# A hybrid encoder on one core: 4 KB slots cut in halves, score rows without slots of their own in the prompt, eight subtractions moved to GpSimd, another pace for side work

## The chip, the cores and the metric

The kernel runs on one core of a Trainium2 chip. The metric is the time of one execution on the device in microseconds (us), taken as the median of three runs. Lower is better.

## The reference, cut to what matters

Two batches go through the same layer with the same weights: a prompt of 512 tokens and a sample of 1024 tokens, both 1024 wide, in float32.

```python
h = _rmsnorm(x, norm_attn_g)
z = h @ w_in                       # q, k, v and two conv halves: 512 + 256 + 1024 columns
a_out = _window_attn(q, k, v, ...) # 8 heads of 64, blocks of 128 with their neighbours,
                                   # m = max(scores, sink); p = exp(s - m)
                                   # denom = sum(p) + exp(sink - m)
c = ca * sigmoid(cb)
c = silu(_layernorm(_dwconv(c, 31 taps)))
x = x + concat([a_out, c]) @ w_out
h = _rmsnorm(x, norm_ffn_g)
u = _dwconv(h @ w_up, 3 taps)      # 5632 columns
x = x + (silu(u[..., :2816]) * u[..., 2816:]) @ w_down
y = _rmsnorm(x, norm_final_g)
```

## The kernel before, in words

A float32 product is made of three matmuls of rounded parts: each operand is split into a high part (`fp32r`, a cast on ScalarE, L142) and a low part (raw less high, a subtraction on GpSimd or VectorE, L143), and high x high, high x low and low x high are added up in PSUM (`proj`, L249 to L252; `out_half`, L648 to L650; `prod`, L1002 to L1004; down-projection, L1334 to L1336). A matmul here is 128x128 by 128x512.

The stages follow one another on TensorE (PE), with side work between:

- To about 95 us the prompt is normed, transposed and projected (`step(i, 0)`, 14 weight chunks of 128 columns). To about 290 us the sample follows with the same 14 chunks and two halves of 512 tokens each, 48 matmuls a chunk. Beside it runs the side job `prompt()`: the prompt's attention in 8 units (4 blocks, 2 groups of four heads; `scores`, L512 to L530, then `values`, L553 to L579), `conv_norm` for its four blocks (L606 to L631: transposes L612, statistics, a normed copy L618, transposes L624, swish) and its output projection.
- To about 683 us the prompt's FFN up-projection goes on in 22 steps (`ffn_step`; convolution taps on VectorE, L775; gate, L797 to L806, stored in the DRAM tiles `gt`). Its side job `sample()` is the sample's attention, 16 units, then the load and split of w_out in 16 pieces of 128x512 (`load_wo`, `split_wo`), then `conv_norm` of the first blocks.
- To about 830 us follows the sample's output projection (`out_blocks`): per block of 128 tokens two halves of 24 matmuls, an addition (L653), a store of the result (`x1d`, L656), a sum of squares (L659), and `scaled` (L900). The side jobs are 11 `pair_sums`: each loads two tiles of `gt` (L811, L812), makes four sums on GpSimd (L816 to L819) and stores four (L821, `gb`); and `conv_norm` of later blocks and `turned` (transposes of the normed rows, L925; high part L927; low part L878). Then come sums of w_up blocks (`sums_up`, subtractions at L878) and their splits (L988, L878).
- The sample's up-projection (to 1240 us) and down-projection follow.

**What sets the order.** The program is written with generators: `tick()` runs between matmuls and takes the next piece of the first side job whenever `pace["due"]` reaches 1; each tick adds `pace["rate"]`. The rates are the constants in L40 (RB for the in-projection of the sample, RD and RN for the FFN, RE for the output projection). A scheduler then orders the instructions of each engine statically, by its own estimate of the time at which each could run. All DMAs of this case are issued by SyncE's queue (SP), in order.

**Memory.** `Slots` (L60 to L92) hands out fixed places in SBUF by size: 15 q of 4096 bytes, 4 c of 4224, 61 h of 2048, 2 d of 2176 and 32 s of 64, per partition. A tile gets a free slot of the least size that holds it, the one longest free first. A tile of 2048 bytes therefore takes a whole q slot of 4096 when no h or d is free. A slot goes back when the last Python reference to its tile is dropped; the next tile in it waits until the reads and DMAs of the one before have ended.

**Score rows.** `sink_columns` takes four q slots for the whole of an attention (`score_rows`), each for two heads, with the negated sink logit in column 0 of each row. `scores` writes the negated and biased scores behind that column (L514), and the exponential (L523) reads the row with the sink's column, so that its accumulated sum is the denominator. The exponentials go into four tiles `p` that `values` then transposes.

Of the kernel before, what the change touches and what calls it, by code (L numbers as in the profile page):

```python
# [9 lines left out]
F32 = mybir.dt.float32  # L10
# [26 lines left out]

RA, RB, RBO, RD, RN, RE = 1.2, 0.8, 2.5, 0.8, 0.95, 1.4  # L40


CA, CB = 0.9, 0.4
# [4 lines left out]
SCB, SCD = "aapa", "aaap"  # L48


WOP, WOA, DW, DW2 = 1, 5, 2, 2
NE = 2
YN = 2
OB = "uc"
VG = 3
NW = 36
U0 = 2


class Slots:  # L60

    def __init__(self, pool, classes):
        self.pool, self.free, self.n = pool, [], 0
        for kind, (count, size) in classes.items():
            for i in range(count):
                self.free.append((f"{kind}{i}", size))

    def tile(self, shape, dt=F32, nbytes=4, among=None):  # L70
        need = nbytes
        for s in shape:
            need *= s
        fits = [s for s in self.free if s[1] >= need and (among is None or s[0][0] in among)]
        if not fits:
            raise RuntimeError(f"no slot for {need} bytes")
        least = min(s[1] for s in fits)
        slot = next(s for s in fits if s[1] == least)
# [13 lines left out]
        self.slots.free.append(self.slot)  # L92


@with_exitstack
def tile_hybrid_encoder(ctx: ExitStack, tc: tile.TileContext, xs, rel_bias, norm_attn_g, w_in,
                        attn_sink, conv_dw_w, conv_dw_b, conv_ln_g, conv_ln_b, w_out, norm_ffn_g,
# [9 lines left out]
    sb = Slots(big, dict(q=(15, 4096), c=(4, 4224), h=(61, 2048), d=(2, 2176), s=(32, 64)))  # L107
# [388 lines left out]
    def scores(u):  # L496
# [7 lines left out]
        off = (kts[0] - b + 1) * P  # L504
        q = qt.pop(u)
        negm, den = sm(GRP), sm(GRP)
        pr = []
        for j in range(GRP):
            h = kv * GRP + j
            sc = bank("attn")  # L510
            for L in range(2):
                nc.tensor.matmul(sc[:, :nk], q[:, j, :], kt[G["g"], kv][L][:, k0:k0 + nk],  # L512
                                 start=(L == 0), stop=(L == 1))
            nc.vector.tensor_tensor_reduce(  # L514
                out=row_of(h)[:, 1:1 + nk], in0=sc[:, :nk], in1=bias[h][:, off:off + nk], scale=-1.0,
                scalar=nsink[:, h:h + 1], op0=ALU.add, op1=ALU.min, accum_out=negm[:, j:j + 1])
            del sc
            if j == 1:
                yield 0.0

        for j in range(GRP):
            p = sb.tile([1 + 3 * P])
            nc.scalar.activation(p[:, :1 + nk], row_of(kv * GRP + j)[:, :1 + nk], AF.Exp, scale=-1.0,  # L523
                                 bias=negm[:, j:j + 1], accum_out=den[:, j:j + 1])
            pr.append(p)
        nc.vector.reciprocal(den[:], den[:])
        for j in range(GRP):
            eng = (SCB if G["g"] == 0 else SCD)[j]
# [1050 lines left out]
```

## Time and profile before

| what | value |
|---|---|
| median of three runs | 1574.94 us (1573.73 to 1581.71) |
| the profiled execution | 1579.13 us |
| its span, first to last instruction | 1577.3 us |
| mean granted clock of TensorE | 0.982 |
| instructions | 20139 |
| DMA, mean over the span | 144 GB/s |

A timeline row gives start and duration in us, engine, line, operation, tiles (out, then in, by their slot kinds: a, b, c, u and t are PSUM banks on the side of a matmul; q, c, d, h and s are slots in SBUF elsewhere), shape and count; in brackets stands the idle time of the engine ahead of it and what ended that. A row of waits gives the engine with its line, what it waited for, the total in us, how often, and the longest. PE is TensorE, DVE VectorE, ACT ScalarE, POOL GpSimd. A busy PE may run at a lower granted clock.

### The profile page before, as it was taken

The page shows a single profiled execution, that of the slowest core. Times are in us where ns is not written, and L with a number is a line of the kernel's source. Part 1 is how long each engine was busy: PE and PEld are TensorE (multiplying, and loading weights), DVE is VectorE, ACT ScalarE, POOL GpSimd, SP SyncE. Part 2 cuts the span into 40 slices and gives each one's busy share as a digit, 9 for nine tenths or more (in the row PEclk, how much of TensorE's full clock was granted, in tenths as well). Part 3 has the DMA queues.
Part 4 walks back from the last instruction along what each step waited for, and adds up shares of the span by engine and source line. Part 5 has one row for each costly group of instructions (what it writes and reads, how often), then busy time and mean ns, then how long its engine had stood idle before and what let it go on. Part 6 is the DMA issues. An engine that isn't in the chain of part 4 may idle for free. (4 is left out here: it accounts for less than half of the span.)

```text
span 1577.3 us, 20139 instructions
## 1 busy us (share of the span) xinstructions
PE 1517.2 (96%) x6843; PEld 1234.2 (78%) x6843; DVE 1155.5 (73%) x1604; ACT 794.6 (50%) x1396; POOL 711.6 (45%) x558
## 2 busy tenths in 40 slices
PE   8999999799999999899979999999999999999997
PEld 6787778587888888788867888888888788888885
DVE  7998577747888895745776787778876945668883
ACT  4635545435677786624344444544445533343354
POOL 6641334324667765746533555555555000003345
PEclk9999899899999999999989999999999999999999
DMA  7573235328343435778432333333331582356644
GB/s 227 159 193 94 69 107 160 100 96 252 105 129 127 131 124 160 222 231 273 147 110 67 99 103 100 101 100 100 105 119 57 191 303 77 117 158 221 216 151 160
DMA packets 228780, 227.17 MB, mean 144 GB/s; under 512 B 13268, under 2 KB 168348, under 8 KB 228549
## 3 DMA queue, kind: packets, MB, share of 16 engines
q1 hardware_dynamic: 228677, 225.88, 45.2%
q8 instruction: 54, 0.88, 0.2%
q14 instruction: 49, 0.40, 0.1%
HBM read 164.74 MB, written 62.14 MB: 144 GB/s over the span
## 5 line engine op out<-in xcount | busy, mean ns | idle before, releaser
L143 POOL TENSOR_TENSOR q<-q,q 128x1024 fp32r<-128x1024 f32 x71 | 172.2, 2431 | 115.4 <-ACT q L142 43.0
L878 DVE TENSOR_TENSOR h<-h,h 128x512 fp32r<-128x512 f32 (+2 forms) x202 | 155.9, 805 | 64.4 <-ACT h L882 25.6
L878 POOL TENSOR_TENSOR q<-q,q 128x512 fp32r<-128x512 f32 x82 | 114.2, 1404 | 152.9 <-ACT q L988 147.7
L1334 PE MATMUL w<-h,h 128*128 128x512 f32 x462 | 181.3, 392 | 0.5 <-DVE q L1121 0.5
L1335 PE MATMUL w<-h,h 128*128 128x512 f32 x462 | 181.3, 392 | 0.0
L1336 PE MATMUL w<-h,h 128*128 128x512 f32 x462 | 181.2, 392 | 0.0
L249 PE MATMUL u<-h,q 128*128 128x512 f32 x400 | 162.4, 406 | 6.5 <-DVE h L775 4.5
L250 PE MATMUL u<-h,q 128*128 128x512 f32 x400 | 159.6, 399 | 0.0
L252 PE MATMUL u<-h,q 128*128 128x512 f32 x384 | 152.4, 397 | 1.9 <-POOL q L143 1.8
L1002 PE MATMUL w<-h,q 128*128 128x512 f32 x372 | 147.7, 397 | 3.5 <-ACT h L1083 1.6
L1004 PE MATMUL w<-h,q 128*128 128x512 f32 x372 | 147.1, 395 | 0.6 <-POOL q L878 0.6
L292 DVE SCALAR_TENSOR_TENSOR c<-c,cvw,c 128x512 f32<-128x512 f32 x184 | 137.9, 750 | 2.5
L875 POOL TENSOR_TENSOR q<-q,q 128x1024 f32<-128x1024 f32 x12 | 32.9, 2752 | 236.9 <-DVE q L875 220.2
L1003 PE MATMUL w<-h,q 128*128 128x512 f32 x350 | 137.7, 393 | 0.0
L882 ACT CAST h<-h 128x512 fp32r<-128x512 f32 x120 | 71.8, 619 | 95.4 <-DVE h L878 41.2
L249 PE MATMUL b<-h,q 128*128 128x512 f32 x256 | 103.7, 405 | 1.9 <-DVE d L322 1.6
L142 ACT CAST q<-q 128x1024 fp32r<-128x1024 f32 x72 | 75.3, 1050 | 59.5 <-DMA q<-in_w_in 23.9
L1334 PEld LDWEIGHTS w<-h,h 128*128 128x128 f32 x462 | 86.8, 188 | 20.5 <-ACT h L882 0.9
L250 PE MATMUL b<-h,q 128*128 128x512 f32 x256 | 102.1, 399 | 0.0
L1336 PEld LDWEIGHTS w<-h,h 128*128 128x128 f32 x462 | 86.7, 188 | 19.6
L1335 PEld LDWEIGHTS w<-h,h 128*128 128x128 f32 x462 | 86.8, 188 | 19.5
L252 PE MATMUL b<-h,q 128*128 128x512 f32 x240 | 95.9, 400 | 0.0
(427 smaller groups left out, 3819.5 us busy)
## 6 DMA issues: line engine op xcount, KB each, us to landing
q<-in_w_up SPq DMA_DIRECT2D x88, 512.0 KB
ga<-q SPq DMA_DIRECT2D x64, 256.0 KB
h<-ga SPq DMA_DIRECT2D x57, 256.0 KB
q<-in_w_in SPq DMA_DIRECT2D x28, 512.0 KB
h<-in_w_down SPq DMA_DIRECT2D x52, 256.0 KB
q<-in_x_sample SPq DMA_DIRECT2D x15, 512.0 KB
h<-qsd SPq DMA_DIRECT2D x24, 256.0 KB
x1d<-q SPq DMA_DIRECT2D x11, 512.0 KB
```

What stands on the lines that cost most here:

```text
L143: (nc.vector if dve else nc.gpsimd).tensor_tensor(lo[:], raw[:], hi[:].bitcast(F32), op=ALU.subtract)
L249: nc.tensor.matmul(out, whi[:, kc, :], hi[:], start=(kc == 0), stop=False)
L250: nc.tensor.matmul(out, whi[:, kc, :], lo[:], start=False, stop=False)
L252: nc.tensor.matmul(out, wlo[:, kc, :], hi[:], start=False, stop=(kc == KC - 1))
L292: nc.vector.scalar_tensor_tensor(acc[:], src(t), w(t), acc[:], op0=ALU.mult, op1=ALU.add)
L878: (eng or nc.vector).tensor_tensor(out, a, b, op=ALU.subtract)
L1002: nc.tensor.matmul(out, whi[:, s], hi[:], start=(start and c == 0), stop=False, **go)
L1003: nc.tensor.matmul(out, whi[:, s], lo[:], start=False, stop=False, **go)
L1004: nc.tensor.matmul(out, wlo[:, s], hi[:], start=False, stop=(stop and c == 3), **go)
L1334: nc.tensor.matmul(out, sh[:, c], th[:], start=(p == 0), stop=False)
L1335: nc.tensor.matmul(out, sh[:, c], tl[:], start=False, stop=False)
L1336: nc.tensor.matmul(out, sl[:, c], th[:], start=False, stop=(p == NPAIR - 1))
```

## The change

Four things are changed.

1. **Halves.** When a 4-byte tile of at most 2048 bytes finds no free slot below 4096 bytes, a free q slot is cut into two `Half` tiles, if more than three q slots (`KEEP`) are free; else it takes a whole slot as before. Free halves are kept by type (`F32`, `F32R`), the last one freed is given out first, and the slot goes back when both are free.
2. **Score rows.** `sink_columns` is called for the sample's attention alone. In the prompt's, the scores go straight into the tile `p`, the exponential runs in place, and the sink's share is made apart: an addition of sink and negated maximum, an exponential (both 128x4) and an addition to the sum.
3. **DW2 = 0.** Of the 16 low parts of the sample's w_out, 8 were on VectorE (`m % 4 < 2`); now all 16 are on GpSimd.
4. **Pace.** The output projection of the sample's first four blocks (i = 4 to 7) runs with rate 2.2 and the next ones with RE = 0.9, where RE = 1.4 held throughout.

```diff
-RA, RB, RBO, RD, RN, RE = 1.2, 0.8, 2.5, 0.8, 0.95, 1.4
+RA, RB, RBO, RD, RN, RE = 1.2, 0.8, 2.5, 0.8, 0.95, 0.9
...
-WOP, WOA, DW, DW2 = 1, 5, 2, 2
+WOP, WOA, DW, DW2 = 1, 5, 2, 0
...
+KEEP = 3
...
+        if self.halved and nbytes == 4 and need <= 2048 and not any(s[1] < 4096 for s in fits):
+            halves = self.halves[dt]
+            if not halves and sum(s[0][0] == self.halved for s in fits) > self.keep:
+                slot = next(s for s in fits if s[0][0] == self.halved)
+                self.free.remove(slot)
+                self.n += 1
+                whole = Whole(self, slot, dt, self.pool.tile([P, 2, 512], dt, tag=slot[0], name=f"{slot[0]}_{self.n}", bufs=1))
+                halves += [(whole, 0), (whole, 1)]
+                whole = None
+            if halves:
+                return Half(*halves.pop(0), shape)
...
+class Half:
...
+    def __del__(self):
+        w = self.whole
+        w.out -= 1
+        if w.out:
+            w.slots.halves[w.dt].append((w, self.i))
+        else:
+            w.slots.halves[w.dt] = [h for h in w.slots.halves[w.dt] if h[0] is not w]
+            w.slots.free.append(w.slot)
...
+        lasting = bool(score_rows)
...
+            if lasting:
+                p = row_of(h)
+            else:
+                p = sb.tile([1 + 3 * P])
+                pr.append(p)
             nc.vector.tensor_tensor_reduce(
-                out=row_of(h)[:, 1:1 + nk], in0=sc[:, :nk], in1=bias[h][:, off:off + nk], scale=-1.0,
+                out=p[:, 1:1 + nk], in0=sc[:, :nk], in1=bias[h][:, off:off + nk], scale=-1.0,
                 scalar=nsink[:, h:h + 1], op0=ALU.add, op1=ALU.min, accum_out=negm[:, j:j + 1])
...
+        else:
+            es = sm(GRP)
+            nc.vector.tensor_tensor(es[:], sinkb[:, kv * GRP:(kv + 1) * GRP], negm[:], op=ALU.add)
+            for j in range(GRP):
+                nc.scalar.activation(pr[j][:, 1:1 + nk], pr[j][:, 1:1 + nk], AF.Exp, scale=-1.0,
+                                     bias=negm[:, j:j + 1], accum_out=den[:, j:j + 1])
+            nc.scalar.activation(es[:], es[:], AF.Exp)
+            nc.vector.tensor_tensor(den[:], den[:], es[:], op=ALU.add)
...
     def prompt():
-        sink_columns()
         yield from attention(0, 8, {u: conv_norm(u - 4) for u in range(4, 8)})
-        kt.clear(), vt.clear(), qt.clear(), bias.clear(), score_rows.clear()
+        kt.clear(), vt.clear(), qt.clear(), bias.clear()
...
+    pace.update(rate=2.2)
     for i in range(4, NB - 2):
         if i + NE < NB:
             side.appendleft(conv_norm(i + NE))
         if i == 8:
+            pace.update(rate=RE)
             side.appendleft(turned(1, old_bank))
```

Where the instructions stand now. In the rows below a name is the slot or its kind (h18 or h, q, a, b, u), the running number of the tile and a further number (h18_231_1392 is the 231st tile, in slot h18); line numbers are those of each kernel, so the projection's L249, L250 and L252 of before are L296, L297 and L299 after, L512 is L560, L553 is L616 and L567, L568 are L630, L631.

PE, in the prompt's attention, beside the sample's first projection chunks; before:

```order
651 L512 MATMUL u0_83_1534<-h55_155_901,h12_231_1390 128x384
652 L512 MATMUL u0_83_1534<-h56_156_902,h12_231_1390 128x384
653 L553 MATMUL u0_89_1613<-ident_75,h18_234_1418 128x128
654 L553 MATMUL u0_89_1613<-ident_75,h17_235_1420 128x128
655 L553 MATMUL u0_89_1613<-ident_75,h13_236_1422 128x128
656 L553 MATMUL u0_89_1613<-ident_75,h14_237_1424 128x128
657 L512 MATMUL a2_92_1686<-h45_153_895,h11_247_1507 128x384
658 L512 MATMUL a2_92_1686<-h54_154_896,h11_247_1507 128x384
659 L512 MATMUL u1_95_1701<-h45_153_895,h11_247_1507 128x384
660 L512 MATMUL u1_95_1701<-h54_154_896,h11_247_1507 128x384
661 L553 MATMUL a0_86_1571<-ident_75,h18_234_1418 128x128
662 L553 MATMUL a0_86_1571<-ident_75,h17_235_1420 128x128
```

And after:

```order
645 L616 MATMUL u0_89_1614<-ident_75,h18_231_1392 128x128
646 L616 MATMUL u0_89_1614<-ident_75,h17_232_1397 128x128
647 L616 MATMUL u0_89_1614<-ident_75,h13_233_1410 128x128
648 L616 MATMUL u0_89_1614<-ident_75,h14_234_1415 128x128
649 L630 MATMUL a0_79_1461<-h11_238_1457,h22_162_954 128x512
650 L631 MATMUL a0_79_1461<-q0_239_1458,h22_162_954 128x512
651 L560 MATMUL a2_84_1540<-h55_155_901,h12_228_1385 128x384
652 L560 MATMUL a2_84_1540<-h56_156_902,h12_228_1385 128x384
653 L296 MATMUL b0_90_1629<-h37_83_525,q13_241_1472 128x512
654 L297 MATMUL b0_90_1629<-h38_84_526,q13_241_1472 128x512
655 L299 MATMUL b0_90_1629<-h37_83_525,q11_242_1473 128x512
656 L296 MATMUL b0_90_1629<-h39_85_541,q13_241_1472 128x512
```

Before, 28 pieces of attention follow one another from row 651 to row 678; after, 22 matmuls of the next projection chunk (rows 653 to 674) stand behind the first of them, and 27 rows without a projection follow later (685 to 711). At about 220 us the new order has 15 to 20 projection matmuls where none stood between transposes and values; at about 270 to 290 us it has 48 ahead of the chain of `conv_norm` and attention and none inside, where 12 stood inside.

POOL, where w_out is split (128x512 from h) beside the w_up chunks of the FFN (128x1024 from q); before:

```order
258 L143 TENSOR_TENSOR h_1031_6432<-h_1021_6396,h_1030_6431 128x512
259 L143 TENSOR_TENSOR q_1037_6452<-q_1013_6366,q_1036_6451 128x1024
260 L805 TENSOR_TENSOR h_1016_6373<-h_1016_6373,h_1012_6362 128x512
261 L143 TENSOR_TENSOR q_1082_6627<-q_1059_6528,q_1081_6626 128x1024
262 L143 TENSOR_TENSOR q_1057_6519<-q_1017_6378,q_1056_6518 128x1024
263 L579 TENSOR_TENSOR h_990_6219<-h_1011_6349,h_1010_6348 64x512
264 L143 TENSOR_TENSOR h_1068_6564<-h_1046_6490,h_1067_6563 128x512
```

And after:

```order
259 L190 TENSOR_TENSOR h_1021_6493<-h_994_6399,h_1020_6492 128x512
260 L190 TENSOR_TENSOR q_983_6353<-q_968_6245,q_982_6352 128x1024
261 L190 TENSOR_TENSOR h_1038_6558<-h_1011_6462,h_1037_6557 128x512
262 L190 TENSOR_TENSOR h_1008_6449<-h_991_6386,h_1007_6448 128x512
263 L190 TENSOR_TENSOR h_1030_6524<-h_1006_6446,h_1029_6523 128x512
264 L190 TENSOR_TENSOR h_999_6416<-h_989_6380,h_998_6415 128x512
265 L867 TENSOR_TENSOR h_984_6357<-h_984_6357,h_980_6346 128x512
266 L642 TENSOR_TENSOR h_958_6203<-h_979_6333,h_978_6332 64x512
267 L190 TENSOR_TENSOR q_1025_6503<-q_985_6362,q_1024_6502 128x1024
268 L190 TENSOR_TENSOR q_1050_6611<-q_1027_6512,q_1049_6610 128x1024
```

The eight that come from VectorE stand among GpSimd's own and ahead of the w_up parts in rows 267 and 268.

SP, at the end of the pair sums (`gb3_10` is a store of the eleventh and last pair, `x1d8` to `x1d11` are the results of the last four blocks); before:

```order
385 L821 DMA gb3_10_3474<-h42_1253_7565 128x256
386 L952 DMA q9_5_8159<-in_w_up 128x8x128
387 L821 DMA gb7_9_3506<-h7_1248_7550 128x256
388 L821 DMA gb5_9_3484<-h7_1248_7550 128x256
389 L821 DMA gb6_9_3495<-h49_1246_7548 128x256
390 L656 DMA x1d10_1175<-q7_1256_7584 128x1024
391 L821 DMA gb3_9_3473<-h45_1249_7551 128x256
392 L656 DMA x1d11_1176<-c2_1259_7618 128x1024
```

And after:

```order
387 L883 DMA gb6_10_3480<-h7_1173_7258 128x256
388 L661 DMA h42_1192_7393<-catd_150 128x512
389 L883 DMA gb3_10_3458<-h55_1176_7261 128x256
390 L661 DMA h7_1193_7394<-catd_150 128x512
391 L661 DMA h8_1208_7446<-catd_150 128x512
392 L719 DMA x1d8_1173<-q1_1180_7306 128x1024
393 L178 DMA q1_1224_7568<-in_x_sample 128x1024
394 L719 DMA x1d9_1174<-q7_1203_7432 128x1024
395 L1014 DMA q3_5_8142<-in_w_up 128x8x128
396 L1014 DMA q0_6_8144<-in_w_up 128x8x128
397 L719 DMA x1d10_1175<-q1_1224_7568 128x1024
398 L719 DMA x1d11_1176<-c1_1227_7602 128x1024
```

Before, the stores of pair 9 are issued beside the last two blocks; the tile that `sums_up` makes for the second w_up chunk was given slot h49, whose tile before is the one that `gb6_9` stores (row 389). After, all stores of the pairs are issued ahead of `x1d8`, that tile is given a slot that no store of a pair holds then, and 21 matmuls stand between the last product of the output projection and the first transposes of the turned rows.

More of the change, by code (lines that the diff above doesn't have):

```diff
@@ L92, in __del__, with __init__, __getitem__ @@
         self.slots.free.append(self.slot)
+class Whole:
+    def __init__(self, slots, slot, dt, t):
+        self.slots, self.slot, self.dt, self.t, self.out = slots, slot, dt, t, 0
+class Half:
+    def __init__(self, whole, i, shape):
+        self.whole, self.i = whole, i
+        whole.out += 1
+        n = 1
+        for d in shape:
+            n *= d
+        ap = whole.t[:, i, 0:n]
+        if len(shape) == 2:
+            ap = ap.rearrange("p (a b) -> p a b", a=shape[0])
+        self.t = ap
+    def __getitem__(self, i):
+        return self.t[i]
+    def __del__(self):
[6 more added lines that the diff above has]
+            w.slots.free.append(w.slot)
 @with_exitstack
@@ L519, in scores @@
                 yield 0.0
[L521 to L525, printed above, removed]
+        if lasting:
+            for j in range(GRP):
+                p = sb.tile([1 + 3 * P])
+                nc.scalar.activation(p[:, :1 + nk], row_of(kv * GRP + j)[:, :1 + nk], AF.Exp, scale=-1.0,
+                                     bias=negm[:, j:j + 1], accum_out=den[:, j:j + 1])
+                pr.append(p)
+        else:
+            es = sm(GRP)
+            nc.vector.tensor_tensor(es[:], sinkb[:, kv * GRP:(kv + 1) * GRP], negm[:], op=ALU.add)
+            for j in range(GRP):
+                nc.scalar.activation(pr[j][:, 1:1 + nk], pr[j][:, 1:1 + nk], AF.Exp, scale=-1.0,
+                                     bias=negm[:, j:j + 1], accum_out=den[:, j:j + 1])
+            nc.scalar.activation(es[:], es[:], AF.Exp)
+            nc.vector.tensor_tensor(den[:], den[:], es[:], op=ALU.add)
         nc.vector.reciprocal(den[:], den[:])
```

5 lines of the change are left out of this document (3 added, 2 removed).

## The prediction

> **What bounds the kernel now.** I read the page first: the busy times, then the slices.
>
> ```profile
> PE 1517.2 (96%) x6843; PEld 1234.2 (78%) x6843; DVE 1155.5 (73%) x1604; ACT 794.6 (50%) x1396; POOL 711.6 (45%) x558
> ...
> PE   8999999799999999899979999999999999999997
> ...
> PEclk9999899899999999999989999999999999999999
> ```
>
> TensorE is busy for 96% of the span, so no other engine bounds the kernel as a whole. The change removes none of its large matmuls. All that can be won is time in which PE is idle, or at a lower granted clock. The slices show where: the few digits below 9, most of which have a lower digit of PEclk too. So I asked for windows of 20 us around those places, with two stretches of heavy DMA and a steady one at the end.
>
> ```profile
> 120.00:140.00 20.00, 18.85 (x93) 15.30 (x92) 15.71 (x36) 11.04 (x31) 4.25 (x3) 1.00 0.29 90
> 140.00:160.00 20.00, 16.87 (x81) 13.35 (x80) 19.70 (x40) 12.49 (x28) 4.86 (x4) 0.96 0.35 100
> 160.00:180.00 20.00, 17.66 (x66) 13.77 (x66) 13.15 (x24) 10.39 (x24) 5.03 (x4) 0.79 0.26 71
> 220.00:240.00 20.00, 16.77 (x73) 13.04 (x72) 14.06 (x28) 13.47 (x31) 7.35 (x7) 0.83 0.62 162
> 260.00:280.00 20.00, 16.80 (x82) 13.37 (x80) 13.66 (x20) 6.33 (x11) 8.72 (x13) 1.00 0.44 118
> 280.00:300.00 20.00, 13.43 (x42) 9.54 (x42) 15.35 (x23) 10.22 (x20) 7.08 (x6) 0.66 0.47 134
> 640.00:660.00 20.00, 18.01 (x83) 14.40 (x81) 14.04 (x17) 14.15 (x24) 13.55 (x9) 1.00 0.91 282
> 660.00:680.00 20.00, 17.45 (x64) 13.78 (x65) 14.85 (x15) 8.38 (x13) 16.01 (x9) 0.83 0.52 173
> 700.00:720.00 20.00, 19.65 (x92) 15.70 (x91) 8.29 (x10) 6.01 (x14) 12.20 (x19) 1.00 0.97 324
> 720.00:740.00 20.00, 20.00 (x100) 16.50 (x99) 10.80 (x16) 5.79 (x12) 11.37 (x18) 1.00 0.90 287
> 780.00:800.00 20.00, 17.84 (x82) 14.39 (x81) 11.38 (x14) 4.71 (x8) 14.65 (x17) 1.00 0.49 164
> 800.00:820.00 20.00, 14.13 (x70) 11.43 (x70) 17.69 (x25) 10.50 (x20) 7.79 (x6) 0.75 0.16 52
> 1400.00:1420.00 20.00, 20.00 (x89) 16.35 (x88) 10.82 (x17) 7.73 (x13) 0.00 (x0) 1.00 0.49 152
> ```
>
> The columns are the window's length, the busy time of PE, PEld, DVE, ACT and POOL, the granted clock, the DMA share and GB/s. I count a window's loss as 20 less PE's busy time, plus 20 times what the clock lacks of 1. For 160 to 180 that is 2.34 + 4.2 = 6.5 us, for 1400 to 1420 nothing. By places: 120 to 180 (prompt attention starts beside the sample's in-projection) 1.2 + 3.9 + 6.5 = 11.6 us; 220 to 240, 6.6; 260 to 300, 3.2 + 13.4 = 16.6; 640 to 680 (w_out is split) 2.0 + 6.0 = 8.0; 780 to 820 (end of the output projection) 2.2 + 10.9 = 13.1. Together 55.9 us can be reached by the four edits, all before 830 us; behind that the order of the work is the same but for names. The waits of PE say who ends the idle time:
>
> ```profile
> PE a L567 <- ACT h L555: 8.1, 4, 5.7
> PE t L925 <- DVE h L878: 5.6, 1, 5.6
> ...
> PE u L624 <- DVE q L618: 2.9, 1, 2.9
> ```
>
> **The change, part by part.**
>
> **Score rows and halves, 120 to 180 us.** The prompt's attention no longer holds four 4 KB slots, and 2 KB tiles share one, so the weight splits of the in-projection come earlier on ACT, and PE has projection matmuls left to put between the pieces of attention.
>
> ```profile
> 156.09 0.66 PE L553 MATMUL u<-ident,h 128*128 128x128 f32 x4 [2.29 <-DVE s L514]
> ...
> 175.34 0.63 PE L252 MATMUL b<-h,q 128*128 128x512 f32 x1
> ...
> 178.72 0.39 PE L250 MATMUL b<-h,q 128*128 128x512 f32 x1
> ```
>
> ```profile
> 157.68 1.05 ACT L142 CAST q<-q 128x1024 fp32r<-128x1024 f32 x1 [0.89 <-DMA ksd<-q]
> ```
>
> At 157.68 ACT makes the high part of the next weight chunk only after a store of keys has left its slot. PE, out of weights, takes 28 attention pieces in a row and waits for their softmax. A stall costs more than itself: the matmuls from 175.34 to 178.72 come 0.42 us apart where the steady window has 20/89 = 0.22, so 8 of them lose 1.6 us. In the new order 22 projection matmuls (4.9 us) stand within that block, yet its last 27 rows are still bare attention, and the softmax behind them is no shorter. Of 11.6 us I take 4.5, a bit under the cover; the ends are 0 (the bare rows wait as long) and 9.
>
> **220 to 240 us.** 15 to 20 projection matmuls now stand where none stood, 3.4 to 4.5 us of cover for 3.2 us of idle time and 3.4 of clock. I take 3, between 0 (the cover stands where PE did not wait) and 6.
>
> **260 to 300 us.** Here the chain of attention and conv_norm is what PE waits for (L624 2.9, L567 5.7). Before, 12 projection matmuls stood inside it; now 48 stand ahead of it and none inside. Cover is lost in one place and the chain starts earlier by it in another. I take 0, with 5 either way.
>
> **Extra small operations.** Each of 8 units gains two DVE and one ACT instruction on 128x4. The nearest row is the reciprocal beside them:
>
> ```profile
> L526 DVE RECIPROCAL s<-s x8: 160/174/179, 125.7 to 258.9; 128x4 f32<-128x4 f32 x8
> ```
>
> Three at 0.17 make 0.5 us a unit, 4 us if all lay on PE's path; most lie under projection matmuls. I take 1, from 0 to 4.
>
> **w_out's low parts on GpSimd, 640 to 680 us.** The rows are those of DVE, POOL and PE, from their timelines:
>
> ```profile
> 652.19 4.41 DVE L143 TENSOR_TENSOR h<-h,h 128x512 fp32r<-128x512 f32 x1
> ...
> 658.63 0.68 DVE L143 TENSOR_TENSOR h<-h,h 128x512 fp32r<-128x512 f32 x1
> ...
> 659.89 7.99 DVE L143 TENSOR_TENSOR h<-h,h 128x512 fp32r<-128x512 f32 x4
> ```
>
> ```profile
> 652.41 2.38 POOL L143 TENSOR_TENSOR q<-q,q 128x1024 fp32r<-128x1024 f32 x1
> 654.76 1.29 POOL L143 TENSOR_TENSOR h<-h,h 128x512 fp32r<-128x512 f32 x1
> 659.98 2.83 POOL L143 TENSOR_TENSOR q<-q,q 128x1024 fp32r<-128x1024 f32 x1 [3.93 <-ACT q L142]
> ...
> 675.35 6.31 POOL L143 TENSOR_TENSOR h<-h,h 128x512 fp32r<-128x512 f32 x5 [3.91 <-ACT h L142]
> ```
>
> ```profile
> 660.12 0.77 PE L249 MATMUL u<-h,q 128*128 128x512 f32 x1 [2.11 <-DVE h L775]
> ...
> 670.32 0.77 PE L249 MATMUL u<-h,q 128*128 128x512 f32 x1 [2.43 <-DVE h L775]
> ```
>
> A low part takes DVE 0.68 us while POOL stands still and 4.41 while POOL subtracts: that one ends at 656.60, right after POOL's two (656.05). Four in a row take 7.99. The convolution taps (L775) stand behind them in DVE's queue, and PE waits twice for those, 2.11 and 2.43 us. With the eight on POOL the taps come sooner, and both waits and most of the low clock behind them can go. The price is on POOL: 8 x 1.29 = 10.3 us more, in a stretch (644 to 682) where its waits of 3.93 and 3.91 us are the idle time that is left. Behind these splits in its queue stand low parts of w_up (2.4 us each), for which PE's next up-projection waits. Of 8.0 us I take 4; the ends are 7 and a loss of 4 (the 10.3 us less the two waits is 2.5, and 1.6 of clock behind it).
>
> The Trainium skill, SBUF — State Buffer, section "Who interferes with whom", says that a DVE instruction with two SBUF inputs and a GpSimd instruction that reads SBUF shut each other out for a whole instruction, whoever starts first. The 4.41-us row agrees. By that rule more POOL work would also hold up DVE's other two-input work, but a tap reads one input from PSUM, so the rule by itself would make this term about 7 instead of 4.
>
> **Pace of the pair sums, 690 to 830 us.** At rate 2.2 all pair sums and their stores are through before the last four blocks; before, the last of them end beside the last blocks.
>
> ```profile
> 795.76 1.33 DVE L878 TENSOR_TENSOR h<-q 128x512 f32<-128x512 f32 x1 [7.82 <-DMA gb<-h]
> ...
> 800.74 0.67 DVE L653 TENSOR_TENSOR c<-c,c 128x512 f32<-128x512 f32 x1
> ...
> 805.14 3.41 DVE L900 SCALAR_TENSOR_TENSOR q<-c,rs,q 128x512 f32<-128x512 f32 x2 [0.72 <-POOL rs L127]
> ```
>
> ```profile
> 799.07 0.66 PE L925 MATMUL b<-ident,q 128*128 128x128 f32 x4 [2.16 <-DVE h L878]
> ...
> 809.80 0.69 PE L925 MATMUL t<-ident,q 128*128 128x128 f32 x2 [5.62 <-DVE h L878]
> ```
>
> The first sum of w_up's second chunk gets the slot of a pair's tile, and so waits until its store has landed: DVE stands for 7.82 us with the whole chain of the last blocks (adding, scaling, row sums) behind it, and PE then waits 2.16 and 5.62 us for the row sums. In the new order that sum's slot is free long before, and 21 matmuls (4.7 us) stand in front of the turned rows. What is late next is that chain itself: the last block's add (0.67), its scalings (3.41) and a sum, which I estimate at 0.7 like the add: 4.8 us from its last matmul, nearly all of it under the 4.7. Of 13.1 us I take 9, from 4 (half of the chain still shows) to 12.
>
> **What the earlier pair sums push on, 690 to 760 us.** Four pairs (two loads of 256 KB and four stores of 128 KB, 1 MB each) move ahead into a stretch that moves 324 and 287 GB/s at shares of 0.97 and 0.90. 4 MB at 324 GB/s are 13 us. SP issues in order, and behind them stand the loads for conv_norm of the last blocks and the first w_up chunks. PE is full there now (19.65 and 20.00 of 20). I take a loss of 3, from 0 (the loads stay a block ahead of their use) to 8.
>
> **Sum.** -4.5 - 3 + 0 + 1 - 4 - 9 + 3 = -16.5 us. Against the profiled execution, 1579.1 us, that gives 1562.6. The median of the runs lies 4.2 us below that execution (1574.94), so I forecast 1558.
>
> **The rivals.**
>
> *The stalls only move.* For it: the bare block in the prompt's attention remains, the chain at 260 to 300 has lost its cover, and POOL is nearly full at 640 to 682. Then the first three terms give 0, w_out 0, the end of the output projection 5, against 1 and 3 for the small operations and the transfers: about 1 us of gain, 1574. Against it: a wait for a slot (7.82 us) that has no reason left.
>
> *The halves hold back the weights.* A 4 KB slot that is cut in two comes back only when both halves are done; a pair of softmax rows then keeps a slot from the weight chunks of the sample's in-projection.
>
> ```profile
> q<-in_w_in SPq DMA_DIRECT2D x28, 512.0 KB
> ```
>
> A chunk feeds 48 matmuls there, 48 x 20/89 = 10.8 us. SP's queue is in order, so one load that waits for a slot holds the later ones too. If two chunks come late by one chunk's time each, PE waits 21.6 us, with some 4 us of low clock; the first two terms are lost, and the rest (0 + 1 - 4 - 9 + 3) stays: +16.6, 1591. It decides from about 17 us of waits, where the rest of the gain is eaten up by 8. Against it: four slots are freed and at least three whole ones are kept.
>
> *The slots free nothing that PE waited for.* Then only the pace and the low parts count: -4 - 9 + 3 + 1 = -9, 1566. For it: ACT's wait for a slot at 157.68 was only 0.89 us; the softmax was the long one.
>
> **How the numbers follow.** The measurement of this kernel can tell about 0.5% (7.9 us) from no change: faster is below 1567, slower above 1582.8. Chances: forecast 0.61, with a range of its own from 1546 to 1567; slots that free nothing 0.08, faster as well; moved stalls 0.20; halves that hold back weights 0.11. So faster 0.69, same 0.20, slower 0.11. The terms at their good ends give -9 - 6 - 5 - 7 - 12 = -39, which they will hardly do all at once; three quarters of that, -29, set the low end, 1545. The high end takes in the moved stalls with the transfers at their bad end (8 for 3), 1579.
>
> **What would show it.** Right: no wait of DVE for a store of pair sums near 795 and PE's waits at L925 under 2 us in sum; no wait of an up-projection matmul for the taps at 640 to 680, with POOL nearly without idle time from 644 to 682 and no new wait for w_up's low part; a granted clock of 0.9 or more in 160 to 180; 260 to 300 as before. The forecast is wrong if PE waits for conv_norm's loads or rows between 700 and 780, if weight chunks come late between 100 and 290, or if the losses turn up again under another line in the same places.

## The result, and the profile after

The changed kernel takes 1560.63 us in the median of four runs (1558.91 to 1564.43), the kernel before 1576.01 beside it. The ratio is 0.9899, with a 95% interval from 0.9876 to 0.9922: about 16 us faster (15.4 by the medians). The forecast was 1558. The profiled execution has a span of 1557.1 us (1577.3 before) and a mean granted clock of 0.990.

The page of the changed kernel, its busy times and slices:

```profile
PE 1506.9 (97%) x6843; PEld 1229.4 (79%) x6843; DVE 1126.2 (72%) x1604; ACT 795.4 (51%) x1404; POOL 708.9 (46%) x566
...
PE   8899998999999999899999999999999999999997
...
PEclk9999999999999999999999999999999999999999
```

The two 7s of PE at a fifth and at half of the span have gone, and the clock is at 9 tenths or more in every slice. The same windows as in the prediction, with two more in the third stage (length, busy time of PE, PEld, DVE, ACT and POOL, granted clock, DMA share, GB/s):

```profile
120.00:140.00 20.00, 17.93 (x90) 15.11 (x91) 17.61 (x43) 9.36 (x28) 1.85 (x2) 1.00 0.27 86
140.00:160.00 20.00, 17.89 (x79) 14.12 (x78) 19.04 (x39) 10.83 (x25) 8.21 (x5) 0.93 0.29 81
160.00:180.00 20.00, 17.70 (x89) 14.18 (x88) 13.45 (x34) 14.68 (x35) 7.39 (x7) 0.99 0.27 78
220.00:240.00 20.00, 19.84 (x95) 15.96 (x94) 13.85 (x27) 11.75 (x25) 9.67 (x8) 1.00 0.49 125
260.00:280.00 20.00, 13.03 (x54) 10.47 (x53) 9.20 (x15) 8.55 (x17) 9.06 (x10) 0.74 0.40 125
280.00:300.00 20.00, 20.00 (x87) 16.11 (x87) 16.87 (x23) 8.13 (x14) 5.12 (x3) 1.00 0.59 173
640.00:660.00 20.00, 15.91 (x62) 12.36 (x61) 6.58 (x9) 10.66 (x17) 19.84 (x14) 0.91 0.78 247
660.00:680.00 20.00, 20.00 (x90) 16.30 (x90) 5.19 (x8) 2.68 (x4) 8.22 (x8) 1.00 0.46 142
680.00:700.00 20.00, 17.81 (x82) 14.46 (x81) 10.39 (x16) 8.70 (x20) 12.10 (x17) 0.91 0.92 316
700.00:720.00 20.00, 20.00 (x95) 16.43 (x94) 10.14 (x15) 6.77 (x14) 14.23 (x22) 1.00 0.86 280
720.00:740.00 20.00, 18.55 (x89) 14.87 (x88) 6.82 (x10) 5.57 (x11) 14.29 (x20) 1.00 0.97 320
740.00:760.00 20.00, 18.32 (x91) 14.74 (x90) 14.81 (x23) 6.57 (x13) 8.58 (x14) 1.00 0.47 160
780.00:800.00 20.00, 19.78 (x107) 15.71 (x107) 15.65 (x23) 10.17 (x18) 5.75 (x8) 1.00 0.22 79
800.00:820.00 20.00, 19.47 (x107) 15.68 (x106) 10.51 (x18) 11.29 (x21) 6.37 (x5) 1.00 0.37 106
```

Loss is counted as in the prediction (idle time of PE plus 20 us times what the clock lacks of 1). At 780 to 820 it fell from 13.1 to 0.8 us, at 220 to 240 from 6.6 to 0.2, at 260 to 300 from 16.6 to 12.2. Around w_out's split it moved rather than fell: at 640 to 660 it rose from 2.0 to 5.9, with VectorE's busy time down from 14.04 to 6.58 and GpSimd's up to 19.84 of 20; at 660 to 680 the 6.0 of before are gone; at 680 to 700, where before lost nothing, it is 4.0. At 720 to 760 there are 3.1 us that were not there. The window of the kernel before that the prediction does not show:

```profile
680.00:700.00 20.00, 20.00 (x93) 16.33 (x92) 9.26 (x14) 6.10 (x11) 7.48 (x10) 1.00 0.54 172
```

The waits of PE in the changed kernel name the lines (L296 is the projection, L687 the second transposes of conv_norm, L711 the output projection, L987 the turned rows; L837 the taps, L681 conv_norm's normed copy, L630 the attention's values):

```profile
PE u L296 <- DVE h L837: 4.1, 2, 3.5
PE u L687 <- DVE q L681: 4.0, 1, 4.0
PE u L687 <- DVE h L681: 2.9, 1, 2.9
...
PE u L711 <- DVE s L678: 2.2, 1, 2.2
...
PE a L630 <- ACT h L618: 0.8, 1, 0.8
...
PE t L987 <- DVE h L940: 0.6, 2, 0.5
```

The wait of 8.1 us for the attention's casts has shrunk to 0.8 and that of 5.6 us at the turned rows to 0.6; the wait for the taps (4.5 before) is there again with 4.1. The 2.2 us at L711 are a wait for taps too: the bank that this matmul takes comes free with a tap that ran from 684.07 to 684.80 on VectorE, and the statistics (L678), which the view names, ended only 0.09 us later.

### The profile page after: what moved, and what is told of

Its sections match the earlier page's. It is cut to its first block, busy times and chain, and to the rows that moved or that the text cites. A ratio compares the mean times of both kernels' runs of the same rounds, so it can differ in the third digit from the quotient of the medians.

```text
span 1557.1 us, 20112 instructions
## 1 busy us (share of the span) xinstructions
PE 1506.9 (97%) x6843; PEld 1229.4 (79%) x6843; DVE 1126.2 (72%) x1604; ACT 795.4 (51%) x1404; POOL 708.9 (46%) x566
## 5 line engine op out<-in xcount | busy, mean ns | idle before, releaser
L940 POOL TENSOR_TENSOR q<-q,q 128x512 fp32r<-128x512 f32 x101 | 140.0, 1391 | 164.0 <-ACT q L1050 151.7
L1064 PE MATMUL w<-h,q 128*128 128x512 f32 x448 | 176.5, 394 | 1.0 <-ACT h L1147 0.6
L1066 PE MATMUL w<-h,q 128*128 128x512 f32 x448 | 175.5, 392 | 1.0 <-POOL q L940 1.0
L1065 PE MATMUL w<-h,q 128*128 128x512 f32 x426 | 166.4, 391 | 0.0
L296 PE MATMUL u<-h,q 128*128 128x512 f32 x400 | 161.0, 403 | 5.4 <-DVE h L837 4.1
L297 PE MATMUL u<-h,q 128*128 128x512 f32 x400 | 158.6, 397 | 0.0
L299 PE MATMUL u<-h,q 128*128 128x512 f32 x384 | 151.8, 395 | 2.7 <-POOL q L190 2.7
L296 PE MATMUL b<-h,q 128*128 128x512 f32 x256 | 102.7, 401 | 3.3 <-DVE d L369 2.2
L837 DVE SCALAR_TENSOR_TENSOR h<-u,fw,h 128x511 f32<-128x511 f32 x88 | 65.5, 744 | 49.8 <-ACT h L841 49.0
L299 PE MATMUL b<-h,q 128*128 128x512 f32 x256 | 101.4, 396 | 0.0
L297 PE MATMUL b<-h,q 128*128 128x512 f32 x256 | 101.1, 395 | 0.0
```

The source lines that it names most:

```text
L296: nc.tensor.matmul(out, whi[:, kc, :], hi[:], start=(kc == 0), stop=False)
L297: nc.tensor.matmul(out, whi[:, kc, :], lo[:], start=False, stop=False)
L299: nc.tensor.matmul(out, wlo[:, kc, :], hi[:], start=False, stop=(kc == KC - 1))
L940: (eng or nc.vector).tensor_tensor(out, a, b, op=ALU.subtract)
L1064: nc.tensor.matmul(out, whi[:, s], hi[:], start=(start and c == 0), stop=False, **go)
L1065: nc.tensor.matmul(out, whi[:, s], lo[:], start=False, stop=False, **go)
```

## The experiments

Twelve kernels were run, each timed against the kernel before in five rounds on the same chip. The table gives the ratio with its 95% interval, and the loss by places in the profiled execution of each, summed over windows of 20 us by the same rule.

| kernel | ratio | 120-180 | 220-260 | 260-300 | 340-420 | 640-700 | 700-780 | 780-840 |
|---|---|---|---|---|---|---|---|---|
| before | 1 | 11.6 | 6.6 | 16.6 | 1.8 | 7.9 | 0.4 | 13.3 |
| changed | 0.9899 (0.9876-0.9922) | 8.1 | 0.9 | 12.2 | 1.9 | 9.9 | 3.1 | 0.8 |
| pace alone | 0.9937 (0.9918-0.9955) | 8.1 | 7.0 | 17.0 | 2.3 | 9.8 | 3.4 | 0.5 |
| low parts alone | 1.0048 (1.0034-1.0061) | 9.9 | 5.4 | 16.8 | 2.3 | 9.1 | 10.3 | 14.1 |
| rows alone | 0.9953 (0.9934-0.9971) | 3.5 | 9.6 | 1.0 | 9.3 | 8.1 | 2.7 | 13.1 |
| halves alone | 0.9927 (0.9910-0.9944) | 10.0 | 6.7 | 8.7 | 2.9 | 3.2 | 0.2 | 15.2 |
| rows and halves | 0.9908 (0.9891-0.9924) | 8.1 | 0.8 | 12.2 | 1.5 | 4.6 | 2.6 | 14.8 |
| changed without low parts | 0.9893 (0.9873-0.9912) | 11.3 | 0.9 | 12.7 | 1.5 | 3.7 | 3.9 | 6.8 |
| low parts, pairs ahead | 0.9969 (0.9958-0.9981) | 11.1 | 5.5 | 14.3 | 1.6 | 9.8 | 1.8 | 6.7 |
| changed without low parts, pairs ahead | 0.9891 (0.9867-0.9915) | 8.0 | 0.8 | 12.0 | 1.8 | 1.6 | 7.5 | 1.6 |
| changed, w_out loaded early | 0.9939 (0.9925-0.9953) | 10.6 | 1.2 | 13.3 | 1.5 | 13.8 | 5.2 | 1.2 |
| changed, low parts all on VectorE | 0.9928 (0.9912-0.9943) | 8.7 | 1.3 | 13.7 | 2.6 | 9.0 | 5.0 | 7.1 |
| changed, pairs ahead | 0.9936 (0.9917-0.9955) | 10.4 | 1.2 | 12.4 | 2.2 | 7.6 | 8.7 | 1.2 |
| rows and halves, sums' tiles held | 0.9924 (0.9908-0.9940) | 13.9 | 0.8 | 13.3 | 2.0 | 2.9 | 8.9 | 5.2 |

Up to some 600 us the order of the instructions on TensorE and VectorE is the same in four of these kernels (before, pace alone and the two with low parts on the kernel before) and the same in eight others (the changed kernel and all that hold rows and halves together). So the early columns are repeated executions of two orders.

**Pace alone.** The kernel before with

```diff
+    pace.update(rate=2.2)
...
+            pace.update(rate=RE)   # RE = 0.9
```

> The kernel before with the new pace alone (2.2 for the first four blocks, 0.9 behind). Theory of places: each edit acts only where its own instructions stand, so this gives the end of the output projection (780 to 840 us, 10 us less loss) and pays 3 us between 700 and 780 for transfers that come together: 7 us faster than before, ratio 0.9955, and no DVE wait for a store of pair sums near 795 us. Rival, luck of slots: the wait went only because the other edits gave the sum's tile another slot; then the wait of some 8 us stands again near 795 us and the time is that of before, ratio 1.000. The prediction's terms for this part were -9 and +3.

Measured: ratio 0.9937, 10 us. The loss at 780 to 840 went from 13.3 to 0.5 and that at 700 to 780 from 0.4 to 3.4, as the theory of places has it. No wait of VectorE for a store of pair sums is left there. The rows of the windows of this kernel, where those of before had 17.84 and 14.13 of PE:

```profile
780.00:800.00 20.00, 20.00 (x97) 16.53 (x96) 17.04 (x23) 7.56 (x14) 9.78 (x8) 1.00 0.25 79
800.00:820.00 20.00, 19.69 (x121) 16.18 (x121) 17.20 (x26) 13.44 (x25) 5.06 (x5) 1.00 0.24 78
```

The rival (luck of slots) falls.

**Low parts alone.** The kernel before with `DW2 = 0`.

> The kernel before with all 16 low parts of the sample's w_out on GpSimd, nothing else changed. The prediction's term: 4 us faster (ratio 0.9975), from the two waits of PE for the convolution taps that stood behind VectorE's stretched subtractions. Theory of places, read from the changed kernel's trace: those two waits go, but PE waits as long for taps that stand behind something else (ScalarE's casts of w_out, which wait for their transfers, ahead of the copy that frees the PSUM bank): 2 us slower, ratio 1.001, with the loss in 640 to 700 us at about 11 us instead of 9.

Measured: ratio 1.0048, 7.7 us slower, more than either theory had. The loss at 640 to 700 rose by 1.2 us only: PE waits 4.5 us for taps, as long as in the kernel before, so of the second theory this half came true. Another 9.9 us came up at 700 to 780, where nothing was moved. There are two new waits of PE there; this is the larger one, followed back through the timelines of PE, VectorE and GpSimd of this kernel:

```profile
751.24 1.12 PE L624 MATMUL a<-ident,h 128*128 128x128 f32 x4 [3.38 <-DVE h L618]
```

```profile
746.77 1.75 DVE L896 SCALAR_TENSOR_TENSOR q<-q,rs,q 128x1024 f32<-128x1024 f32 x1 [5.83 <-POOL rs L127]
...
750.38 0.81 DVE L618 TENSOR_SCALAR h<-a,s,s 128x512 f32<-128x512 f32 x1 [0.72 <-POOL s L127]
```

```profile
744.79 0.74 POOL L816 TENSOR_TENSOR h<-h,h 128x256 f32<-128x256 f32 x1 [3.73 <-DMA h<-gt]
...
746.18 0.56 POOL L127 TENSOR_TENSOR rs<-rs,nhalf 128x1 f32<-128x1 f32 x1
```

GpSimd stands 3.73 us for a pair's tile; the small instruction that makes a block's rstd (one over a root, by which the block's rows are scaled) is two rows behind in its queue; VectorE stands 5.83 us for that rstd, with the rest of conv_norm's chain behind; PE stands for conv_norm's copy.

**Rows alone.** Lasting score rows in the sample's attention only, no halves:

```diff
-    sb = Slots(big, dict(...), "q", KEEP)
+    sb = Slots(big, dict(...))
```

> The kernel before with score rows that last in the sample's attention alone; no halves, pace and low parts as before. Theory of slots: the four 4 KB slots that come free for the weight chunks are what counts, so this alone brings most of the 12 us that the changed kernel loses less between 120 and 300 us: 8 us faster, ratio 0.995. Rival, halves: without them the 2 KB tiles of the attention go on taking whole 4 KB slots, and the four freed ones are used up by them: at most 3 us faster, ratio 0.998 or more.

Measured: ratio 0.9953, 7.5 us, as the theory of slots has it in sum. By places it is another picture: 260 to 300 fell to 1.0 and 120 to 180 to 3.5, while 220 to 260 rose to 9.6 and 340 to 420 to 9.3, where PE waits at the start of the FFN for a transposed row's high part:

```profile
PE u L296 <- ACT h L257: 5.1, 1, 5.1
```

**Halves alone.** Halves, with `sink_columns()` called in `prompt()` as before.

> The kernel before with 4 KB slots cut in halves, but lasting score rows in both attentions, pace and low parts as before. Theory of slots: four slots stay with the score rows, so halves alone bring little, 2 to 4 us, ratio 0.998. Rival, halves: they are what keeps slots free for the weights, and this alone brings most of the 12 us: 8 us faster or more, ratio 0.995 or less.

Measured: ratio 0.9927, 11 us, by the ratio the largest of the four edits taken singly (its interval overlaps that of the pace alone); the rival has it. Of the loss, 7.9 us went at 260 to 300, which the expectation meant, and 4.7 us at 640 to 700, which it did not. There PE waits 1.1 us for the taps instead of 4.5, and VectorE's eight low parts, which stand among the taps, take 10.4 us instead of 14.5. I put this down to the 2 KB tiles that the sample's attention and w_out's pieces both take there; no run isolates that. The wait and the windows of this kernel there (its taps are L838), against 18.01 and 17.45 of PE and a clock of 0.83 before:

```profile
PE u L296 <- DVE h L838: 1.1, 1, 1.1
```

```profile
640.00:660.00 20.00, 18.88 (x87) 15.22 (x86) 13.69 (x16) 16.11 (x25) 14.99 (x9) 1.00 0.75 226
660.00:680.00 20.00, 17.93 (x82) 14.44 (x81) 9.77 (x15) 5.09 (x8) 14.09 (x11) 1.00 0.66 211
```

**Rows and halves.** Both, with pace and low parts as before.

> Score rows and halves together, pace and low parts as before. Theory of places: the changed kernel's loss between 100 and 420 us is 11 us below that of before, and this kernel has the same instructions there, so it is 11 us faster than before, ratio 0.993. That is less than rows alone and halves alone add up to, because both free slots for the same weight chunks. Rival, they add up: 7.5 + 11 = 18 us, ratio 0.9885.

Measured: ratio 0.9908, 14.5 us, between the two: they do not add up (18.5). In this profile the loss fell by 14.0 us between 120 and 420 and by 3.3 at 640 to 700, and rose by 3.7 behind that.

**Changed without the low parts.** `DW2 = 2` in the changed kernel.

> The changed kernel with the 8 low parts back on VectorE. Theory of places: the move by itself cost 7.6 us, so without it the score rows, the halves (11 us) and the pace (10 us) remain: 21 us faster than before, ratio 0.987, 5 us below the changed kernel. Rival, the prediction's term: the move gains 4 us in company, where pace and slots have changed what stands behind it; then this is slower than the changed kernel by 4 us, ratio 0.9925.

Measured: ratio 0.9893, against 0.9899 with them. Neither theory: in company the move shows neither cost nor gain, within intervals of 3 to 4 us either way. The places show two shares against each other. With the low parts on GpSimd the loss at 640 to 700 is 9.9, without 3.7; at 780 to 840 it is 0.8 with them and 6.8 without. The wait of PE there is on a scaling of the last block, whose rstd stands in GpSimd's queue behind a low part that waited for ScalarE; PE, then GpSimd of this kernel:

```profile
794.44 0.47 PE L987 MATMUL t<-ident,q 128*128 128x128 f32 x1 [3.21 <-DVE q L962]
```

```profile
791.43 1.27 POOL L940 TENSOR_TENSOR q<-h,q 128x512 fp32r<-128x512 f32 x1 [6.79 <-ACT q L1050]
...
793.05 0.55 POOL L174 TENSOR_TENSOR rs<-rs,nhalf 128x1 f32<-128x1 f32 x1
```

**Pairs ahead, with the low parts on the kernel before.**

```diff
+        for r in (p, p + 1):
+            if r < NPAIR and r not in pair_in:
+                pair_in[r] = sb.tile([NT]), sb.tile([NT])
+                for n in range(2):
+                    nc.sync.dma_start(pair_in[r][n][:], gt[2 * r + n][:])
+        e, o = pair_in.pop(p)
```

> The kernel before with all 16 low parts on GpSimd, as in the run of that part alone, and in addition each pair's two tiles loaded one pair ahead of its sums. Theory of GpSimd's line: in that run 10 us of the loss came between 700 and 780 us, where a pair's sums stood in GpSimd's queue waiting for their load, with the two small rstd instructions of the blocks behind them; with the tiles there earlier that goes: about 9 us faster than that run, ratio to before 0.999. Rival, transfers: the load comes late because the queues of DMA are full then, and asking earlier changes nothing; ratio 1.005 as in that run.

Measured: ratio 0.9969 against 1.0048 without tiles ahead: 12 us. At 700 to 780 the loss fell from 10.3 to 1.8, as expected, so GpSimd's wait for the pairs was the cause there. Another 7.4 us went at 780 to 840, where the pairs now end earlier; that was not expected.

**Pairs ahead, changed kernel without low parts, and changed kernel.** The same edit in two more kernels.

> The changed kernel with the 8 low parts back on VectorE and each pair's tiles loaded one pair ahead. Theory of GpSimd's line: the 3 us that the pace costs between 700 and 780 go too: 24 us faster than before, ratio 0.985. Rival: with rate 2.2 the pairs' transfers already come together, two more tiles in flight take slots from w_up and conv_norm, and nothing is won: ratio 0.987 or more.

> The changed kernel with each pair's two tiles loaded one pair ahead. Theory of GpSimd's line: the 6 us of loss between 700 and 780 fall to 3, 3 us faster than the changed kernel, ratio 0.988. Rival: at rate 2.2 the stretch is bound by its transfers (shares of 0.9 and more), so the loads come no earlier and PE waits for conv_norm's own loads; no gain, ratio 0.990, as with the low parts on VectorE (0.9891 with tiles ahead, 0.9893 without).

Measured: 0.9891 without the low parts (0.9893 without tiles ahead), and 0.9936 in the changed kernel itself, 6 us slower than that, though the intervals (0.9917 to 0.9955 and 0.9876 to 0.9922) touch. At 700 to 780 the loss rose to 7.5 and 8.7. The rivals have the times: nothing is won. Their reason, that what is in flight more is in the way, is not shown: PE's waits for conv_norm's loads in that stretch are 4.2 us with tiles ahead against 3.1 without (no low parts), and 3.0 against 1.4 (changed kernel), which is only a part of what the loss rose by.

**w_out loaded early.** `WOA` 9 instead of 5 in the changed kernel.

> The changed kernel with each piece of w_out loaded 9 steps ahead of its split instead of 5. Theory of ScalarE's line: in the changed kernel PE waits 4.1 us at 650 to 656 for taps, because ScalarE casts w_out pieces in order, stands up to 1.4 us for their loads (4.8 us in 600 to 690), and the copy that frees PE's bank is behind them. With earlier loads these waits of ScalarE fall under 1.5 us in sum, PE's to under 1.5, the loss of 635 to 700 us from 11 to about 7: 4 us faster than the changed kernel, ratio 0.9875. Rival, GpSimd full: it has 16 low parts and the w_up parts to make there in either case, and PE waits as long: ratio 0.990.

Measured: ratio 0.9939, 6 us slower than the changed kernel. The expectation failed at its first step: ScalarE's wait for w_out's pieces grew. Between 600 and 690 us it was, in the changed kernel and in this one:

```profile
ACT h L189 <- DMA h<-in_w_out: 4.8, 5, 1.4
```

```profile
ACT h L189 <- DMA h<-in_w_out: 7.7, 3, 4.8
```

So it does not tell what the wait costs; only that asking earlier for these loads did not make them land before their casts.

**Low parts all on VectorE.** `DW2 = 4` in the changed kernel.

> The changed kernel with all 16 low parts of w_out on VectorE and none on GpSimd. Theory of the shared way into SBUF (VectorE's subtractions stretch while GpSimd subtracts, 4.41 us for one in the profile of before): 16 of them ahead of the taps make PE wait there as in the kernel before or longer, loss of 635 to 700 us 9 to 14, ratio 0.992 or more. Rival, order: with the halves there is room for the order to put them between the taps, and with GpSimd free of low parts of w_out nothing stretches: loss about 5 as with 8 of them on VectorE, ratio 0.989 or less.

Measured: ratio 0.9928, loss at 640 to 700 9.0 us, and PE waits 5.6 us for the taps: the first theory has the time and the place. That the subtractions stretch has less support. The group of the 16 subtractions in this kernel (least, median and greatest duration in ns) shows most of them at their short time:

```profile
L190 DVE TENSOR_TENSOR h<-h,h x16: 678/693/3156, 630.8 to 668.6; 128x512 fp32r<-128x512 f32 x16
```

**Rows and halves, the sums' tiles held.** Taken before the pair sums, so in no slot of a pair:

```diff
+    third_sum.update((j, sb.tile([NT])) for j in range(2))
     side.extend(pair_sums(p) for p in range(NPAIR))
```

> Score rows and halves, pace and low parts as before, and the two tiles for the first sums of w_up are taken before the pair sums begin, so that they stand in no slot of a pair. Theory of the slot: VectorE's wait of 7.7 us for a store of pair sums near 780 us is what costs the 16 us of loss at 780 to 845 in the run of the slots alone; without it 8 to 9 us go there, and the 3 us that the pace costs between 700 and 780 are not paid: about 1556 us, ratio 0.985, faster than the changed kernel. Rival, the stores themselves are late: the low parts of the turned rows, a few rows further in VectorE's queue, take slots of the same pairs and wait for their stores in turn; the wait moves there, 4 us at most are won, ratio 0.988 or more.

Measured: ratio 0.9924, by the ratios 2.5 us slower than rows and halves alone, with overlapping intervals. At the place itself the theory of the slot is right: without VectorE's wait of 7.7 us the loss at 780 to 840 fell from 14.8 to 5.2. But 6.3 us came up at 700 to 780, most of it at 700 to 720. The first sum of w_up, freed of its slot, now stands early in VectorE's queue, and waits there for its load with conv_norm's normed copy (L681) behind it; VectorE, then PE of this kernel:

```profile
712.35 0.69 DVE L940 TENSOR_TENSOR h<-q 128x512 f32<-128x512 f32 x1 [3.21 <-DMA q<-in_w_up]
712.96 0.81 DVE L681 TENSOR_SCALAR h<-a,s,s 128x512 f32<-128x512 f32 x1
```

```profile
713.91 1.04 PE L687 MATMUL a<-ident,h 128*128 128x128 f32 x4 [3.80 <-DVE h L681]
```

No version beats the changed kernel beyond the intervals; without low parts it is as fast (0.9893, and 0.9891 with pairs ahead).

## Why the prediction was right, and where it was not

The time, 1560.6 us, is within 3 us of the forecast and inside the narrow range (1546 to 1567). That is partly luck: the mechanism of the largest term, the pace, was right, but the sum came right because gains that were missed or put too low stood against two, 8.5 of the 16.5 us, that did not come.

- **120 to 180 us, forecast -4.5.** Not shown. The profiles give 11.6 before and 8.1 after, but the same order of before gave 11.6, 8.1, 9.9 and 11.1 in four kernels (mean 10.2), and that of the changed kernel 8.1, 8.1, 11.3, 8.0, 10.6, 8.7, 10.4 and 13.9 in eight (mean 9.9). The step that failed is "22 projection matmuls stand within that block": the cover came, yet by the means the loss is what it was, so the 27 bare rows behind it seem to cost as much as the block had, the lower end that the text gave.
- **220 to 260, forecast -3.** 6.1 to 1.0 in the same means, -5.1: right, a little small.
- **260 to 300, forecast 0 with 5 either way.** 16.2 to 12.7, -3.5: the chain that starts earlier wins over the lost cover, though PE now waits 4.0 and 2.9 us for conv_norm, which I take for the cover that is lost. Halves alone (8.7) and rows alone (1.0) end better there than both.
- **Rows and halves at 640 to 700: no term.** The prediction looked for the slots' worth only beside the in-projection. With VectorE keeping its eight low parts, kernels without halves lose 7.9, 9.8 and 8.1 there, those with halves 3.2, 4.6, 3.7, 1.6 and 2.9: about -5.4. This is what the forecast missed most. PE's wait for the taps is 4.5, 6.4 and 4.5 us in the first three, and 1.1 or nothing in the other five, where the eight subtractions take about 10 us instead of 14 to 15. So the wait that the next term was to take away does go, by the halves.
- **Low parts on GpSimd, forecast -4.** Wrong. Alone it is +7.7, in company nothing. The step that failed is that "the taps come sooner, and both waits" go. VectorE did become free (6.58 of 20 us busy), yet PE waits for the taps as long as before, since the taps come late for another reason and PE has less to do until they do. In the changed kernel, PE, VectorE, ScalarE and GpSimd:

```profile
651.59 0.47 PE L296 MATMUL u<-h,q 128*128 128x512 f32 x1 [0.64 <-DVE h L837]
651.90 0.40 PE L297 MATMUL u<-h,q 128*128 128x512 f32 x1
655.75 0.76 PE L296 MATMUL u<-h,q 128*128 128x512 f32 x1 [3.45 <-DVE h L837]
...
664.00 0.40 PE L299 MATMUL u<-h,q 128*128 128x512 f32 x1
```

```profile
654.07 1.53 DVE L837 SCALAR_TENSOR_TENSOR h<-u,fw,h 128x511 f32<-128x511 f32 x2 [0.52 <-ACT h L841]
```

```profile
651.70 0.62 ACT L189 CAST h<-h 128x512 fp32r<-128x512 f32 x1 [1.32 <-DMA h<-in_w_out]
652.23 0.59 ACT L861 ACTIVATE b<-h 128x512 f32<-128x512 f32 x1
652.76 0.60 ACT L189 CAST h<-h 128x512 fp32r<-128x512 f32 x1
653.26 0.77 ACT L841 ACTIVATE h<-u,vecs,fw 128x512 f32<-128x512 f32 x1
```

```profile
650.45 6.99 POOL L190 TENSOR_TENSOR q<-q,q 128x1024 fp32r<-128x1024 f32 x3
657.39 8.79 POOL L190 TENSOR_TENSOR h<-h,h 128x512 fp32r<-128x512 f32 x7
```

  The copy that the taps add to (L841) stands third in ScalarE's queue behind a cast that waits for its load; it starts 2.8 us after the last matmul of its bank. (The taps read the bank too, so it comes free with the last tap and not, as two of the expectations have it, with the copy.) PE feels this because of the order: between the two waits it has two matmuls of one w_up group, 651.59 and 651.90, then takes the 24 of the next group, and the other 22 of the first follow only at 664.00. GpSimd makes the low part of that first group last of the three at 650.45. All four kernels with the 16 parts on GpSimd and w_out loaded 5 steps ahead have this order; in each of them PE waits 3.6 to 4.5 us for the taps here, and 2.2 more at the start of the output projection. In the nine that leave 8 or 16 parts to VectorE the low part comes ahead of the other group's, and the 24 matmuls stand together, about 5.4 us of cover. No run isolates the order, and the run with earlier loads, which has yet another order, did not settle what ScalarE's wait costs.

  So the prediction's bound on GpSimd's price (4 us, at w_up's low parts) was nearer than it looks: PE waits for no such part in this stretch, but these parts come later on GpSimd, and the order gives up PE's cover for it. The sign that GpSimd would be nearly without idle time to 682 held to 666 only. When the move was made alone, a larger price came 50 to 100 us later, by the rstds behind the pair sums. The rule of the Trainium skill that was weighed there (SBUF — State Buffer, "Who interferes with whom") would have made the term 7, further off. The 4.41-us row agrees with the rule, but PE's wait in the changed kernel hung on something else.
- **Pace, forecast -9, and the transfers, +3.** Right, by place: pace alone gives 12.8 less at 780 to 840 and 3.0 more at 700 to 780; in the changed kernel it is 12.5 and 2.7. The mechanism (VectorE's wait in a pair's slot) is shown by the run with held tiles, where that loss fell by 9.6 at the place. In company the pace brings less: from rows and halves (0.9908) to both with the pace (0.9893) it is 2.4 us with overlapping intervals. In that profile the rstd of the last block stands behind another wait of GpSimd, which I take for a part of it.
- **Small operations, +1.** Not seen apart; within the early columns.
- **The rivals.** *Halves hold back the weights* falls: halves alone are 11 us faster than before. *The slots free nothing* falls: rows and halves alone bring 14.5 us. *The stalls only move* is not the result, but it is what several of the last experiments did: a wait taken away at one place of 640 to 840 us came up, in part or in full, at another.

By the means of the places the sum is 0 - 5.1 - 3.5 + 0 (640 to 700: -5.4 by the halves, +5.6 by the low parts, the mean of 9.9 and 7.6 with them on GpSimd less 3.2) + 2.7 - 12.5, about -18; the medians say -15.4, the two profiled spans -20.2.

## What to carry to other kernels

Ask of a stalled instruction what is first in its engine's queue, and ask the same of that one's queue: work taken off VectorE helped nothing while the taps waited for ScalarE, and rstd instructions of half a microsecond, behind a load that GpSimd waited for, cost some 9 us. Ask also what the waiting engine has left to do: with the work on GpSimd, TensorE had two matmuls between two waits where it had 24. Memory that comes free can act in stages far from the edit, here 350 us behind it, so look for its worth in all of them. When four edits come together, run each alone: here one that cost 7.7 us by itself, and nothing that can be seen in company, stood among three that gained.

## What was not expected of the hardware

One and the same order of instructions lost between 8.0 and 13.9 us at 120 to 180 us in eight executions, which were taken on several chips, while it lost between 0.8 and 1.3 at 220 to 260. A single profile can't tell a gain of 3 us in the first of these places.
